# A hybrid mLSTM and gated DeltaNet block on one core: the sums of u tied to the weight splits, a quarter of an inverse copied out first and read a step later, one mLSTM head started three steps later

## The chip, the cores and the metric

One core of one Trainium2 chip runs the kernel. The metric is device microseconds from the first to the last work of a launch, the median of several runs. The engines named below are PE (TensorE, matrix products into PSUM banks), DVE (VectorE), ACT (ScalarE), POOL (GpSimd) and SP (SyncE, which here only issues DMAs; ACT issues some too). Each engine works through its own instructions in order and waits on semaphores for the others.

## The reference, cut to what matters

Sequence 512, model width 2048, one layer. A normalised input u is multiplied by one wide weight matrix; its columns feed two token mixers and their gates.

```python
u = _rmsnorm(h, norm_w)
proj = jnp.matmul(u, w_in)          # (512, 2048) x (2048, 20528)
...
h_a = _mlstm_chunkwise(q, k, v, i_pre, logf)          # 8 heads, q/k 128 wide, v 256 wide
h_a = _merge_heads(_rmsnorm(h_a)) * ml_norm_w * sigmoid(ml_o) * silu(ml_z)
...
h_b = _gated_delta_chunkwise(dq, dk_, dv_, beta, g)   # 16 heads, 128 wide
#   per chunk: lhs = I + strict_lower(beta * (k k^T) * decay); sol = lhs^-1 rhs
h_b = _merge_heads(_rmsnorm(h_b, dn_norm_w)) * silu(dn_z)
y = sigmoid(gate_a) * (h_a @ w_out[:2048]) + sigmoid(gate_b) * (h_b @ w_out[2048:])
out = _rmsnorm(x + y, final_norm_w)
```

All of it is float32. The inverse of a unit lower triangular matrix per head and chunk (`lhs`) is what the second part of the change touches.

## The kernel before, in words

**Products in three.** Each float32 operand is split into a high part rounded to the matrix unit's float32r and a low remainder, and a product is three matmuls: high by high, high by low, low by high. u is kept split (`uh`, `ul`). Weights come from memory in steps: `load_raw` (SP) brings `wr`, `split_hi` (ACT, line 135) casts it to `wh`, `split_lo` (DVE, line 138) subtracts to `wl`. Four buffers of each; splits are made three steps ahead (`SAHEAD`), with the priority offset 2 x `PRIO`.

**Order.** PE's instructions stay in the order in which the program writes them. The other engines' are ordered by a scheduler that simulates time: an instruction that is ready may be pulled ahead of ones written earlier, and `urgent(level)` lifts its priority by level x `PRIO`. `behind("V")` and `behind("A")` place an instruction after the newest weight split of DVE or ACT that had been written by then. They add an order on that engine, no semaphore.

**Ticks.** `proj_cm` and `proj_tm` are the projections. After every 6 matmuls of 512 columns (12 of 256 in `proj_tm`) they call `tick()`, which advances a clock by one and lets background generators run: each generator writes some work, yields a number, and comes back that many ticks later. `start(gen, wait)` sets its first tick. So a number in a `yield` or `start` places work between the projection's matmuls. A projection of 256 columns takes 16 ticks.

**First stage.** After the first projection (ML_Q) the generators `gates()`, `u_sums()` (start 9) and `lead()` start, beside ML_K and two narrow gate projections (48 ticks in all; their results leave PSUM by ACT in `spill`, line 369, and `narrow_gates`, line 733, at ticks 16, 32 and 48). `u_sums` runs eight iterations: DVE adds `uh` and `ul` of two row blocks into `X` (line 391), POOL makes four sums and differences (lines 394 to 397), four ticks later ACT casts them to `suh` and `s4h` (line 400) and DVE subtracts to `sul` and `s4l` (line 401), one tick later the next iteration begins. There is one `X`. The sums are read by the next stage.

**Seven products.** A stage of wide projections (`seven`, lines 586 to 588) uses a scheme of seven products in place of eight for 2 x 2 blocks, with `suh`, `sul`, `s4h`, `s4l`, and takes until about 990 us.

**Units.** Eight units then run, each with two DeltaNet heads and, in units 1 to 6, an mLSTM head (`dn_unit`): projections DN_K, for these units the mLSTM's q and k, DN_V and DN_Q, 16 ticks each. Evacuations of the projections' banks (`yp`, line 777) are ACT's. mLSTM heads 0 and 1 have their q and k computed earlier, and `ml_first(0)` and `ml_first(1)` start at ticks 1 and 42 of this stage. A head loads q and k (`mkq`, one buffer), turns k by a DVE transpose and a trip through memory (`turn`, `travel`: four small DMAs out, lines 803 to 818), loads its broadcast rows and v (line 1110, one buffer `v1`), works through four chunks and stores its result to `hm_d` by eight DMAs that ACT issues (line 813).

**The inverse.** `dn_front_k` inverts the 32 x 32 diagonal blocks; `dn_back` joins them for eight matrices at a time (two heads, four chunks):

- p1 (line 944), copied out negated to `s1` by ACT (line 949), two ticks;
- p2 (lines 955 and 956), three groups in one PSUM bank. ACT copies two of them to `tb` (line 960), then DVE copies the third to `ta` (line 962); two ticks;
- p3 (line 966) reads `ta`; ACT negates it to `s3` (line 969); two ticks;
- p4 (line 973) reads `s3` and `tb`; DVE copies it to `tb` (line 975); then two chains (`dn_chain`) start, which run the recurrence with `tb`.

Accesses of different engines to one PSUM bank are ordered one after the other, as written. `dn_back` starts 9 ticks after the unit's last projection, 25 in the units without an mLSTM head.

**End.** Two more gate projections, then the output projection, in which the stored results are read back.

Of the kernel before, what the change touches and what calls it, by code (L numbers as in the profile page):

```python
# [8 lines left out]
F32 = mybir.dt.float32  # L9
F32R = mybir.dt.float32r  # L10
AF = mybir.ActivationFunctionType
ALU = mybir.AluOpType
# [4 lines left out]
S = 512  # L17
# [13 lines left out]
HP = S // 2  # L31
# [24 lines left out]
def hybrid_body(  # L56
# [18 lines left out]
    V, A, G, T = nc.vector, nc.scalar, nc.gpsimd, nc.tensor  # L75
# [64 lines left out]
    def behind(eng):  # L140

        return tc.issue_after(newest[eng])
# [70 lines left out]
    def urgent(level=1):  # L213
        return tc.high_priority(offset=level * PRIO)
# [4 lines left out]
    def start(gen, wait=0):  # L219
        active.append([gen, clock["t"] + wait])  # L220
# [12 lines left out]
    uh = up.tile([P, KT, S], F32R, tag="uh", name="uh")  # L233
    ul = up.tile([P, KT * S + 120], F32R, tag="ul", name="ul")[:, 0:KT * S].rearrange("p (k s) -> p k s", s=S)
# [149 lines left out]
    X = sbp.tile([P, 2, 2, NO], F32, tag="X", name="X")  # L384
    U1, C22 = ([X[:, q, t, :] for t in range(2)] for q in range(2))
    t2_d = dr.tile([2, KH, P, NO], F32, tag="t2d", name="t2_d")

    def u_sums():
        for i in range(KH):
            uf, sf = X[:, 0, :, :], X[:, 1, :, :].rearrange("p a (b n) -> p (a b) n", n=HP)  # L390
            V.tensor_tensor(out=uf, in0=uh[:, 2 * i:2 * i + 2, :].bitcast(F32), in1=ul[:, 2 * i:2 * i + 2, :].bitcast(F32),
                            op=ALU.add)
            a11, a21, a12, a22 = uf[:, 0, 0:HP], uf[:, 0, HP:S], uf[:, 1, 0:HP], uf[:, 1, HP:S]
            G.tensor_tensor(out=sf[:, 0], in0=a21, in1=a22, op=ALU.add)
            G.tensor_tensor(out=sf[:, 1], in0=sf[:, 0], in1=a11, op=ALU.subtract)
            G.tensor_tensor(out=sf[:, 2], in0=a11, in1=a21, op=ALU.subtract)
            G.tensor_tensor(out=sf[:, 3], in0=a12, in1=sf[:, 1], op=ALU.subtract)
            yield 4
            for hi, lo, src in ((suh[:, i], sul[:, i], sf[:, 0:3]), (s4h[:, i], s4l[:, i], sf[:, 3])):
                A.copy(hi, src)  # L400
                V.tensor_tensor(out=lo, in0=src, in1=hi.bitcast(F32), op=ALU.subtract)
            yield 1

    acol = cp.tile([P, NC, MLH], F32, tag="acol", name="acol")
# [314 lines left out]
    def lead():  # L719
        for _ in range(3):  # L720
            load_quad()
            yield 2
        prep_sums(0)
        prep_pair(0)
        yield 1
# [8 lines left out]
            nc.sync.dma_start(tg_d[2 * i:2 * i + 2, :, b * NB:(b + 1) * NB].rearrange("c p n -> p c n"), tg)  # L734

    start(gates())
    start(u_sums(), 9)
    start(lead(), 38)
    spill(proj_cm(ML_K), 2, 1.0)
    for b in range(GFIRST):  # L740
# [20 lines left out]
    ta = wk.tile([64, 2 * NC, 64], F32, tag="ta", name="ta", bufs=1)  # L761
# [8 lines left out]
    def bc(col, n):  # L770
        return col.unsqueeze(2).to_broadcast([P, NC, n])
# [158 lines left out]
    def dn_back(hs, kq, u):  # L930

        tn, tt = u["tn"], u["tt"]
        G2 = [(j * NC + c, u["aq"][j][:, c, 0, :]) for j in range(2) for c in range(NC)]
        for b in range(4):
            bs = slice(b * BS, (b + 1) * BS)
            G.tensor_copy(tb[bs, :, bs], tt[bs])
        for b in range(2):
            bs = slice(b * BS, (b + 1) * BS)
            G.tensor_copy(ta[bs, :, bs], tn[bs])
        p1 = psw.tile([P, 2 * NC, BS], F32, tag="wk", name="p1")  # L940
        for g, a in G2:
            for q in range(2):
                a0, a1 = slice(64 * q, 64 * q + 32), slice(64 * q + 32, 64 * q + 64)
                T.matmul(p1[a1, g, :], a[a0, a1], tn[a0, g, :], start=True, stop=True)
        s1 = wk.tile([P, 2 * NC, BS], F32, tag="s3", name="s1", bufs=1)
        for q in range(2):
            a1 = slice(64 * q + 32, 64 * q + 64)
            with urgent():
                A.mul(s1[a1], p1[a1], -1.0)
        yield 2  # L950
        p2 = psw.tile([P, 2, 2 * NC, BS], F32, tag="wk", name="p2")
        for g, a in G2:
            for q in range(2):
                a0, a1 = slice(64 * q, 64 * q + 32), slice(64 * q + 32, 64 * q + 64)
                T.matmul(p2[a0, 0, g, :], s1[a1, g, :], tt[a1, g, :], start=True, stop=True)
            T.matmul(p2[32:64, 1, g, :], tt[32:64, g, :], s1[32:64, g, :], start=True, stop=True)
        for q in range(2):
            a0, a1 = slice(64 * q, 64 * q + 32), slice(64 * q + 32, 64 * q + 64)
            with urgent():
                A.copy(tb[a0, :, a1], p2[a0, 0])  # L960
        with urgent():
            V.tensor_copy(ta[32:64, :, 0:32], p2[32:64, 1])
        yield 2
        p3 = psw.tile([P, 2 * NC, 64], F32, tag="wk", name="p3")
        for g, a in G2:
            T.matmul(p3[64:128, g, :], a[0:64, 64:128], ta[:, g, :], start=True, stop=True)
        s3 = wk.tile([P, 2 * NC, 64], F32, tag="s3", name="s3", bufs=1)
        with urgent():
            A.mul(s3[64:128], p3[64:128], -1.0)
        yield 2  # L970
        p4 = psw.tile([P, 2 * NC, 64], F32, tag="wk", name="p4")
        for g, a in G2:
            T.matmul(p4[0:64, g, :], s3[64:128, g, :], tb[64:128, g, 64:128], start=True, stop=True)
        with urgent():
            V.tensor_copy(tb[0:64, :, 64:128], p4[0:64])
        for j in range(2):
            vn = u["vs"][j]
            with behind("V"):
                V.tensor_tensor(out=vn, in0=vn, in1=bc(u["nk"][:, j, :], P), op=ALU.mult)
        start(dn_chain(0, hs, kq, u), 2)  # L980
        start(dn_chain(1, hs, kq, u), 3)
# [60 lines left out]
    def dn_unit(p, mh):  # L1042
# [27 lines left out]
        for j in range(2):  # L1070
# [3 lines left out]
            start(silu_end(kq[j][:, 1, :], (kq[j][:, 1, :], qn)), 4 + 3 * j)  # L1074
        start(dn_front_q(hs, kq, u), QWAIT)
        start(dn_back(hs, kq, u), 25 if mh is None else 9)

    def ml_head(h, kq, late):
# [83 lines left out]
    def ml_first(h):  # L1162

        kq = wk.tile([P, 2, S], F32, tag="mkq", name="mkq", bufs=1)
        for i in range(2):
            nc.sync.dma_start(kq[:, 1 - i, :], qk_d[2 * i + h])
        yield 4
        yield from ml_head(h, kq, 0)

    start(ml_first(0), 1)  # L1170
    start(ml_first(1), 42)
    for unit in UNITS:
        dn_unit(*unit)

# [137 lines left out]
def hybrid_block(tc, *args):  # L1312
    with tc.block(schedule_with_timeline_sim=True):
        hybrid_body(tc, *args)
# [25 lines left out]
```

## Time and profile before

| | us |
|---|---|
| median of 3 runs | 2259.2 (2257.6 to 2261.88) |
| the profiled execution, its own time | 2272.74 |
| its span, first to last instruction | 2271.0 |
| PE busy | 2200.4 |
| DVE busy | 1581.6 |
| ACT busy | 917.9 |
| POOL busy | 264.1 |

The page gives one execution under the hardware profiler. "Busy" is the union of an engine's instructions; waiting and the issue of DMAs are not busy. A row of the timeline reads: start in us from the span's start, duration in us, engine and line, operation, what it writes and reads, shape and count, and in brackets the idle time of that engine just before it with what ended it. In the view of waits a row reads: who waited for whom, total us, how often, the longest. A row of the windows gives the stretch, its length, the busy time of PE, of PE's weight loads, of DVE, ACT and POOL with their instruction counts, the clock granted to TensorE, the share of the DMA engines and GB/s. A `q` behind an engine's name is its sequencer, here the issue of a DMA.

### The profile page before, as it was taken

To read this page: it belongs to the slowest core of one execution; us is meant where nothing else is said; L and a number is where in the kernel's file an instruction comes from. 1 tells how busy PE (TensorE), PEld (TensorE's weight loads), DVE (VectorE), ACT (ScalarE), POOL (GpSimd) and SP (SyncE) were. 2 spreads that over 40 slices of the span, in tenths; PEclk is the share of its full clock that TensorE was granted. 3 is DMA by queue.
4 is the path that set the end of the run, shared out by engine and by line. 5 is a ranking of instruction groups with operands and counts; after the bars stand their busy time and mean duration, and the time that the engine had idled before them with its cause. 6 is when DMAs were issued, how large, how long until landed. Compare 5 with 4: busy or idle time off the path is not lost.

```text
span 2271.0 us, 33013 instructions
## 1 busy us (share of the span) xinstructions
PE 2200.4 (97%) x11504; PEld 1842.8 (81%) x11504; DVE 1581.6 (70%) x2793; ACT 917.9 (40%) x1788; POOL 264.1 (12%) x340
## 2 busy tenths in 40 slices
PE   6899999999999999999999999999999999999998
PEld 5887888788778778887888878787878899978886
DVE  5967798788778777757877777776777775444435
ACT  4434444445444444443434334343434434332223
POOL 0500000000000000012312121212121210000111
PEclk9999999999999999999999999999999999999999
DMA  5355666567667766867666665656565566864333
GB/s 158 87 190 184 205 208 209 191 199 229 202 206 220 232 205 201 250 189 186 154 155 160 143 156 140 156 140 150 142 153 141 143 165 181 251 200 148 116 116 130
DMA packets 521385, 397.09 MB, mean 175 GB/s; under 512 B 239873, under 2 KB 408034, under 8 KB 521218
## 3 DMA queue, kind: packets, MB, share of 16 engines
q1 hardware_dynamic: 427778, 341.42, 53.9%
q10 hardware_dynamic: 93440, 53.56, 7.8%
q8 instruction: 90, 1.47, 0.3%
q14 instruction: 77, 0.63, 0.1%
HBM read 318.25 MB, written 76.61 MB: 174 GB/s over the span
## 4 chain that ended last, share of the span: by engine, by line
PE 64%; DMA 17%; DVE 10%; issue 3%; SPq 3%; ACT 2%; POOL 0%; ACTq 0%; DVEq 0%; POOLq 0%
PE pj L258 9%; PE pj L259 9%; PE pj L260 9%; PE ps L587 6%; PE ps L586 6%; PE ps L588 6%; DMA wr<-t_d 5%; DVE wl L138 5%; PE py L1274 3%; PE py L1275 3%; PE py L1273 3%; DMA wr<-in_w_in_dram 3%; DMA hm_d<-to 2%; SPq L512 1%; ACT wh L135 1%
## 5 line engine op out<-in xcount | busy, mean ns | idle before, releaser
L138 DVE TENSOR_TENSOR wl<-wr,wh 128x512 fp32r<-128x512 f32 (+1 forms) x592 | 480.0, 814 | 271.1 <-ACT wh L135 265.6
L135 ACT CAST wh<-wr 128x512 fp32r<-128x512 f32 (+1 forms) x592 | 404.0, 685 | 613.0 <-PE pj L259 240.9
L258 PE MATMUL pj<-uh,wh 128*128 128x512 f32 x1024 | 433.3, 423 | 4.9 <-ACT yp L777 4.9
L260 PE MATMUL pj<-uh,wl 128*128 128x512 f32 x1024 | 404.0, 395 | 0.0
L259 PE MATMUL pj<-ul,wh 128*128 128x512 f32 x1024 | 403.1, 394 | 0.0
L260 PEld LDWEIGHTS pj<-uh,wl 128*128 128x128 f32 x1024 | 194.4, 190 | 44.1
L258 PEld LDWEIGHTS pj<-uh,wh 128*128 128x128 f32 x1024 | 195.4, 191 | 40.9 <-ACT yp L777 5.7
L259 PEld LDWEIGHTS pj<-ul,wh 128*128 128x128 f32 x1024 | 195.7, 191 | 33.5
L587 PE MATMUL ps<-wl,uh 128*128 128x512 f32 x528 | 208.1, 394 | 6.7 <-DVE wl L138 6.5
L586 PE MATMUL ps<-wh,uh 128*128 128x512 f32 x528 | 207.1, 392 | 4.8 <-DVE X L567 4.6
L586 PE MATMUL ps<-wh,suh 128*128 128x512 f32 x528 | 205.8, 390 | 1.4 <-ACT to L626 1.4
L588 PE MATMUL ps<-wh,ul 128*128 128x512 f32 x528 | 205.7, 390 | 0.0
L587 PE MATMUL ps<-wl,suh 128*128 128x512 f32 x528 | 205.5, 389 | 0.0
L588 PE MATMUL ps<-wh,sul 128*128 128x512 f32 x528 | 205.4, 389 | 0.0
L135 ACT CAST wh<-ts 128x512 fp32r<-128x512 f32 x176 | 109.0, 619 | 201.3 <-DVE ts L542 154.4
L135 ACT CAST wh<-t 128x1024 fp32r<-128x1024 f32 x88 | 92.9, 1055 | 196.0 <-PE ps L588 108.6
L273 PE MATMUL pjt<-wh,uh 128*128 128x256 f32 x512 | 148.5, 290 | 4.2 <-ACT tgs L733 2.7
L275 PE MATMUL pjt<-wl,uh 128*128 128x256 f32 x512 | 145.9, 285 | 1.8 <-DVE wl L138 1.8
L276 PE MATMUL pjt<-wh,ul 128*128 128x256 f32 x512 | 145.6, 284 | 0.0
L138 DVE TENSOR_TENSOR wl<-ts,wh 128x512 fp32r<-128x512 f32 x176 | 120.4, 688 | 33.7 <-ACT wh L135 33.7
L138 DVE TENSOR_TENSOR wl<-t,wh 128x1024 fp32r<-128x1024 f32 x88 | 107.8, 1225 | 43.8 <-ACT wh L135 43.2
L587 PEld LDWEIGHTS ps<-wl,uh 128*128 128x128 f32 x528 | 99.1, 188 | 35.1 <-DVE wl L138 16.0
(288 smaller groups left out, 3897.9 us busy)
## 6 DMA issues: line engine op xcount, KB each, us to landing
wr<-in_w_in_dram SPq DMA_DIRECT2D x680, 256.0 KB, 3.7
wr<-in_w_out_dram SPq DMA_DIRECT2D x128, 256.0 KB, 3.1
t_d<-ts ACTq DMA_DIRECT2D x88, 256.0 KB, 3.9
wr<-t_d SPq DMA_DIRECT2D x88, 256.0 KB, 4.1
wr<-in_w_in_dram SPq DMA_DIRECT2D x96, 128.0 KB, 2.8
tgl<-tg_d SPq DMA_DIRECT2D x24, 256.0 KB, 3.9
xt<-in_x_dram SPq DMA_DIRECT2D x8, 512.0 KB, 7.7
v<-v_d SPq DMA_DIRECT2D x8, 512.0 KB, 6.8
```

The costliest lines, as they stand in the source:

```text
L135: newest["A"] = A.copy(hi, src).ins
L138: newest["V"] = V.tensor_tensor(out=lo, in0=src, in1=hi.bitcast(F32), op=ALU.subtract).ins
L258: T.matmul(ps[j], hi[:, k, wsl], uh[:, kt, :], start=(kt == 0), stop=False)
L259: T.matmul(ps[j], hi[:, k, wsl], ul[:, kt, :], start=False, stop=False)
L260: T.matmul(ps[j], lo[:, k, wsl], uh[:, kt, :], start=False, stop=(kt == KT - 1))
L273: T.matmul(o, uh[:, kt, tsl], hi[:, k, :], start=(kt == 0 and c % 2 == 0), stop=False, skip_group_check=True)
L275: T.matmul(o, uh[:, kt, tsl], lo[:, k, :], start=False, stop=False, skip_group_check=True)
L276: T.matmul(o, ul[:, kt, tsl], hi[:, k, :], start=False, stop=(kt == KT - 1), skip_group_check=True)
L586: T.matmul(ps[t], ah, hi, start=(g == "A" and i == 0), stop=False, skip_group_check=True)
L587: T.matmul(ps[t], ah, lo, start=False, stop=False, skip_group_check=True)
L588: T.matmul(ps[t], al, hi, start=False, stop=(i == KH - 1), skip_group_check=True)
L1273: T.matmul(ps[c], hh[base][:, kt, tsl], hi[:, 0, :], start=(kt == 0), stop=False)
```

## The change

Three edits. In `u_sums` the DVE and ACT instructions are put behind the newest weight split of their engine, the views of `X` are made once, and the generator starts at tick 11 in place of 9. In `dn_back` the copy of `ta` is written ahead of ACT's two copies from the same bank, with the priority offset 2 x `PRIO` in place of one, and p3 comes three ticks after p2 in place of two. The second mLSTM head starts at tick 45 in place of 42.

```diff
     def u_sums():
+        uf, sf = X[:, 0, :, :], X[:, 1, :, :].rearrange("p a (b n) -> p (a b) n", n=HP)
+        a11, a21, a12, a22 = uf[:, 0, 0:HP], uf[:, 0, HP:S], uf[:, 1, 0:HP], uf[:, 1, HP:S]
         for i in range(KH):
-            uf, sf = X[:, 0, :, :], X[:, 1, :, :].rearrange("p a (b n) -> p (a b) n", n=HP)
-            V.tensor_tensor(out=uf, in0=uh[:, 2 * i:2 * i + 2, :].bitcast(F32), in1=ul[:, 2 * i:2 * i + 2, :].bitcast(F32),
-                            op=ALU.add)
-            a11, a21, a12, a22 = uf[:, 0, 0:HP], uf[:, 0, HP:S], uf[:, 1, 0:HP], uf[:, 1, HP:S]
+            with behind("V"):
+                V.tensor_tensor(out=uf, in0=uh[:, 2 * i:2 * i + 2, :].bitcast(F32),
+                                in1=ul[:, 2 * i:2 * i + 2, :].bitcast(F32), op=ALU.add)
             G.tensor_tensor(out=sf[:, 0], in0=a21, in1=a22, op=ALU.add)
...
             yield 4
             for hi, lo, src in ((suh[:, i], sul[:, i], sf[:, 0:3]), (s4h[:, i], s4l[:, i], sf[:, 3])):
-                A.copy(hi, src)
-                V.tensor_tensor(out=lo, in0=src, in1=hi.bitcast(F32), op=ALU.subtract)
+                with behind("A"):
+                    A.copy(hi, src)
+                with behind("V"):
+                    V.tensor_tensor(out=lo, in0=src, in1=hi.bitcast(F32), op=ALU.subtract)
             yield 1
...
-    start(u_sums(), 9)
+    start(u_sums(), 11)
...
             T.matmul(p2[32:64, 1, g, :], tt[32:64, g, :], s1[32:64, g, :], start=True, stop=True)
+        with urgent(2):
+            V.tensor_copy(ta[32:64, :, 0:32], p2[32:64, 1])
         for q in range(2):
             a0, a1 = slice(64 * q, 64 * q + 32), slice(64 * q + 32, 64 * q + 64)
             with urgent():
                 A.copy(tb[a0, :, a1], p2[a0, 0])
-        with urgent():
-            V.tensor_copy(ta[32:64, :, 0:32], p2[32:64, 1])
-        yield 2
+        yield 3
         p3 = psw.tile([P, 2 * NC, 64], F32, tag="wk", name="p3")
...
     start(ml_first(0), 1)
-    start(ml_first(1), 42)
+    start(ml_first(1), 45)
```

## The prediction

> **What bounds the kernel now.** I read the page first.
>
> ```profile
> span 2271.0 us, 33013 instructions
> PE 2200.4 (97%) x11504; PEld 1842.8 (81%) x11504; DVE 1581.6 (70%) x2793; ACT 917.9 (40%) x1788; POOL 264.1 (12%) x340
> ```
>
> PE is the bound: of 2271.0 us it idles 70.6. The change removes no matmul, so it can only move PE's waits and what follows from them. Second, PE's waits, longest in total first.
>
> ```profile
> engine line waited for: us in total, times, longest us
> PE p L966 <- DVE ta L962: 13.3, 5, 3.6
> PE pj L258 <- ACT yp L777: 4.9, 1, 4.9
> PE pjt L273 <- ACT tgs L733: 2.7, 1, 2.7
> PE pjt L275 <- DVE wl L138: 1.8, 2, 1.4
> PE pjt L273 <- ACT qk L369: 1.5, 1, 1.5
> ```
>
> L966 is the product p3 of the inverse, which waits for the quarter `ta`. L273 and L275 are the narrow projections that run beside the sums of u. L258 behind L777 is one wait near 1077 us, beside the second mLSTM head. So each part of the change stands beside one of the largest waits. Third, TensorE's granted clock (third figure from the end, 1.00 being full) in windows laid around these waits, and matmul steps from the chain in the second window.
>
> ```profile
> 110.00:118.00 8.00, 5.66 (x29) 5.66 (x30) 3.66 (x9) 3.89 (x8) 0.83 (x2) 0.57 0.58 153
> 1076.00:1084.00 8.00, 6.26 (x16) 4.97 (x17) 6.28 (x15) 4.02 (x9) 0.26 (x1) 0.57 1.11 233
> 1329.00:1333.00 4.00, 4.00 (x12) 2.87 (x10) 1.90 (x3) 0.78 (x2) 0.00 (x0) 0.57 0.77 202
> 1441.00:1446.00 5.00, 5.00 (x22) 3.71 (x19) 1.88 (x4) 1.21 (x2) 0.00 (x0) 0.66 0.91 215
> 1554.00:1562.00 8.00, 7.96 (x43) 6.25 (x44) 2.79 (x5) 1.90 (x4) 0.99 (x1) 0.57 1.01 253
> 1670.00:1674.00 4.00, 4.00 (x21) 3.25 (x19) 0.40 (x2) 1.21 (x2) 0.00 (x0) 0.57 0.93 226
> 1082.80 0.43 PE pj L260
> 1084.25 0.23 PE pj L259
> ```
>
> After each long wait the clock is lowered for a while and a matmul step takes 0.43 us in place of 0.23. A window of 8 us at 0.57 misses 8 x 0.43 = 3.4 us of clock; at half clock a missed microsecond costs (1 - 0.23/0.43)/0.5 = 0.93 us, so 3.2 us. The four windows from 1329 miss 1.7 + 1.7 + 3.4 + 1.7 = 8.5 us: 8.0 us of time. The waits above therefore cost more than their own row tells.
>
> **The quarter that leaves first.** The third product's starts, and the stretch around the second of them:
>
> ```profile
> 1327.36 0.82 PE L966 MATMUL p<-ta,aq 64*64 64x64 f32 x11 [2.77 <-DVE ta L962]
> 1440.42 0.76 PE L966 MATMUL p<-ta,aq 64*64 64x64 f32 x10 [2.89 <-DVE ta L962]
> 1554.04 1.25 PE L966 MATMUL p<-ta,aq 64*64 64x64 f32 x12 [3.44 <-DVE ta L962]
> 1669.60 0.59 PE L966 MATMUL p<-ta,aq 64*64 64x64 f32 x7 [3.60 <-DVE ta L962]
> 1434.39 0.19 PE L956 MATMUL p<-s,tt 32*32 32x32 f32 x1
> 1436.38 1.53 DVE L138 TENSOR_TENSOR wl<-wr,wh 128x512 fp32r<-128x512 f32 x1 [3.07 <-ACT wh L135]
> 1436.81 2.24 ACTq L813 DMA_DIRECT2D hm_d<-to  x3
> 1439.09 0.74 ACT L960 COPY tb<-p 32x256 f32<-32x256 f32 x2 [2.74 <-DMA hm_d<-to]
> 1439.86 0.42 DVE L962 COPY ta<-p 32x256 f32<-32x256 f32 x1 [1.95 <-ACT tb L960]
> ```
>
> p2 is complete at 1434.6. ACT is held in its issues of hm_d, copies tb only at 1439.09, and DVE's copy of ta, from the same bank and later in the program, waits for ACT's two. With ta first, ACT waits for DVE instead. But DVE has a weight split (1436.38 to 1437.91) ahead of it, itself held by ACT; both rank alike for the scheduler and the split is the older, so I leave it first: ta is then done at 1437.91 + 0.42 = 1438.3. PE's place for p3, without the wait, is 1440.42 - 2.89 = 1437.5. The third step of the yield adds one tick, six matmul steps of 0.23, 1.4 us: 1438.9. So p3 finds ta there with 0.6 us to spare; the reorder alone would leave some 0.8 us of wait. The other three units read alike, by their waits. At once behind the tb copies on ACT stand one hm_d issue, a weight cast and s3's evacuation, and p4 waits for the last: p3 ends at 1438.9 + 1.1 = 1440.0 (estimate from 16 products), p4's place is two ticks on, 1442.8, and ACT is done with tb at 1439.83, so after that issue and the cast s3 still has some 1.5 us (estimate). p4, the copy back and the chains all move one tick; PE fills that tick with projection products, so it costs nothing while these last, and 1.4 us at the most behind the last unit, where gate products still run. Removed: 13.3 us of waits plus 8.0 us of lowered clock, 21.3; bounds 8 (half of the waits stay, the clock with them partly) and 21.3. I take 21.
>
> Row against rule: gaps of 2.77 and 2.89 us were each followed by the lowered clock (windows from 1329 and 1441). The Trainium skill (TensorE: Matmul & The Clock Gate, Part 1: The HAM clock gate) has the clock halved after at least one idle window of about 3.4 us, by which these two gaps would have kept the full clock. By that rule alone the sum would be 3.2 us smaller; the trace decides, and I use its windows.
>
> **The sums of u.** First what ACT waited for ahead of line 400, then rows of the timeline:
>
> ```profile
>   POOL X L395: 21.6, 7
> 80.59 0.83 ACT L400 CAST suh<-X 128x768 fp32r<-128x768 f32 x1 [3.81 <-POOL X L395]
> 59.00 0.74 POOL L396 TENSOR_TENSOR X<-X 128x256 f32<-128x256 f32 x1
> 103.93 1.21 DVE L391 TENSOR_TENSOR X<-uh,ul 128x1024 f32<-128x1024 f32 x1
> 106.08 2.66 POOL L394 TENSOR_TENSOR X<-X 128x256 f32<-128x256 f32 x1 [2.62 <-DVE sul L401]
> 110.14 0.83 ACT L400 CAST suh<-X 128x768 fp32r<-128x768 f32 x1 [1.64 <-POOL X L395]
> 111.70 0.59 ACT L733 ACTIVATE tgs<-pjt 128x512 f32<-128x512 f32 x1
> ```
>
> The first row is ACT's idle time ahead of its casts of these sums: seven waits, 21.6 us. They run far ahead of the step that wrote them: the free scheduler pulled them forward, and ACT and DVE, in order, then stand in front of PE's evacuations. At 80.59 that held qk (1.5 us of PE), at 110.14 it held tgs (2.7 us, then the lowered clock of 110 to 118, 3.2 us). Tied to the splits, an iteration starts with its tick (11, 16, ... 46) and casts four ticks later (15, ... 50); the evacuations are at ticks 16, 32 and 48. Four ticks of about 1.4 us are 5.6 us; the slowest iteration shown, DVE add at 103.93 to ACT cast at 110.14, took 6.2, the first POOL sums 0.74 each. So most casts find their data. The DVE, ACT and POOL instructions are the same in number; they end 15 to 20 us later (tick 50 in place of 111), beside the first strips of the seven-product stage, which reads one iteration's sums every four ticks, about 5.5 us, and so the last one's long after tick 50. What is queued behind a tied cast is the next weight cast, and PE waits for that. All that could go: 2.7 + 1.5 + 1.8 + 3.2 = 9.2; it could also give 3 us back at the new overlap (one wait like tgs). I take 6.5: qk, tgs and its clock gone (7.4), the wl waits kept, 0.9 for the overlap.
>
> **The second head.** The timeline around the yp wait, and in the second row the chain:
>
> ```profile
> 1071.24 0.43 SPq L1110 DMA_DIRECT2D v<-v_d  x1
> 1071.24 5.49 DMA v<-v_d
> 1073.21 3.85 ACTq L813 DMA_DIRECT2D hm_d<-to  x2
> 1077.10 0.59 ACT L777 COPY yp<-pj 128x512 f32<-128x512 f32 x1 [5.86 <-DMA v<-v_d]
> 1075.30 4.22 SPq L813 DMA_DIRECT2D td<-kw  x4
> ```
>
> The first head's hm_d issues on ACT wait for the landing of the second head's v, and the evacuation yp stands behind them. Of the second head's transfers on SP, the two mkq loads were issued ahead of this stretch, v goes when the first head frees its buffer, which three ticks (4.1 us) of trace order do not alter, and td of kw, tied to a split, moves to about 1079.4. That takes four transfers out of the stretch, but they were issued after v. All of it could go (4.9 + 3.2 = 8.1), or a wait could arise at the third head, whose one mkq buffer is freed one tick before it is wanted (1.4 us lost). I take 2.
>
> **Sum.** 21 + 6.5 + 2 = 29.5; I take off 2 for waits that newly come up, since everything that ran during the stalls now has less time: 27.5. The profiled execution took 2272.74 us (span 2271.0 and 1.7 around it): 2245 after. The median of the runs shown is 2259.2, 13.5 lower. If these 13.5 lie in PE's 70.6 idle us, the waits are a fifth smaller there and the gain is 22; if not, 27.5. I take 25: 2234.
>
> **Rivals.**
> 1. The wait moves rather than goes: DVE's ta copy stays behind a split whose cast stands behind ACT's hm_d issues. The 0.6 us to spare speaks for it; the tick given as well speaks against it. With 2 us left in each of four units and their clock lowered as now, 21 becomes 5 and the sum 5 + 6.5 + 2 - 2 = 11.5, scaled 10: 2249. Chance 0.18.
> 2. POOL stays as slow where the sums are put: L394 took 2.66 us beside DVE's work and 0.74 is what L396 took, so casts go on waiting. The sums then gain nothing: 27.5 - 6.5 = 21, by the same scaling 19, 2240. Chance 0.14. Beside this: the Trainium skill (SBUF — State Buffer, Who interferes with whom) has a DVE instruction with two SBUF inputs and a GpSimd one that reads SBUF exclude each other for a whole instruction. No row here shows whether it is that lock.
> 3. The second head's three steps do clear the v collision: 8.1 in place of 2, and the wl waits go as well: about 35 by the profile, 32 scaled, 2227. For it: the stretch has fewer transfers; against it: v's issue time. Chance 0.08.
> 4. Slower: the tied casts hold the weight casts on ACT, so PE waits in each of the eight iterations. Like tgs with its clock, 2.7 + 3.2 = 5.9 each, 47; less 9.2 that go and 23 of the other parts: 15 slower, 2274. It decides from (23 + 9.2)/8 = 4.0 us an iteration. A weight cast runs about three steps of 2.7 us (twelve of 0.23) ahead of its use, so POOL would have to end some 8 us later than in the slowest iteration shown, and in every one. Chance 0.05.
>
> **How the numbers follow.** Forecast 0.53 (2222 to 2243), rivals 0.18, 0.14, 0.08, 0.05, and 0.02 that nothing measurable happens. 0.2% (4.5 us) is about what a measurement tells from no change. A part of rival 1 and of rival 2 ends within it: faster 0.87, same 0.07, slower 0.06. The range reaches from all that could go (21.3 + 9.2 + 8.1 = 38.6, less 2 for new waits and unscaled, 37) to a gain of 8, the low bound of the quarter alone: 2222 to 2251.
>
> **What would show it.** L966 behind L962 gone from PE's waits, or under 3 us; the granted clock full near 1330, 1440, 1550 and 1670; ta's copy ahead of tb's; tgs and qk gone from PE's waits and the clock full at 110 to 118; ACT's idle time ahead of L400 well under 21.6. The yp wait near 1075 may stay. Wrong would be: p3 still waiting 2 us or more, p4 (L973) taking its place, or weight splits (L138) as PE's largest wait before 180 us.

## The result, and the profile after

| | before | after |
|---|---|---|
| median, us | 2260.58 (6 runs, 2257.6 to 2268.12) | 2241.63 (6 runs, 2234.45 to 2244.56) |
| ratio, 95% interval | | 0.9904 [0.988, 0.9928] |
| the profiled execution, us | 2272.74 | 2236.92 |
| PE idle in it (span less PE busy), us | 70.6 | 46.9 |

The change makes the kernel 19 us faster by the medians; 25 were forecast, 2234 against 2241.63. The two profiled executions lie 35.9 us apart by their spans, since that of before stands 12 us above its median and that of after 5 below. Of the 35.9, 23.7 are idle time of PE that went (70.6 - 46.9) and 12.2 are busy time (2200.4 - 2188.2) with the same 11504 matmuls. The clock accounts for most of these: the six windows of the prediction miss 15.3 us of clock in all, after has only the yp window below at 0.57 (3.4 us), and 11.9 us at the prediction's 0.93 are 11.1 us of time (estimate). Of the idle time, 19.3 us are the rows at which the change aims (below); another 5.5 are waits in the seven products, to which the paragraph on the sum comes back. The first rows of the page of after:

```profile
span 2235.1 us, 33004 instructions
PE 2188.2 (98%) x11504; PEld 1835.7 (82%) x11504; DVE 1566.5 (70%) x2793; ACT 913.6 (41%) x1788; POOL 271.6 (12%) x340
```

The waits of PE in after (who waited for whom, total us, how often, the longest):

```profile
...
PE pj L258 <- ACT yp L780: 4.5, 1, 4.5
PE ps L589 <- DVE X L570: 2.9, 4, 1.2
PE ps L590 <- DVE wl L138: 2.7, 6, 0.5
```

Lines after the first edit are three higher now: p3 is L969, p4 L976, the evacuation yp L780, the seven products L589 and L590. The wait of p3 for `ta` (13.3 us) is no row any more, nor are `tgs`, `qk` and the weight split of the narrow gates (6.0 together). The yp wait stays. Above it stands only that of the kernel's first product (`pprm`), 15.0 us and 15.1 in before, which the change doesn't touch; below it come waits of a size that before had too. The same places by windows in after (stretch, length, busy PE, PEld, DVE, ACT, POOL, granted clock, DMA share, GB/s): beside the sums, at the yp wait, and round p3 of the four units whose p3 waited longest in before (it now starts at 1307.76, 1417.13, 1526.53 and 1635.06).

```profile
110.00:118.00 8.00, 8.00 (x69) 8.00 (x69) 7.22 (x9) 3.86 (x6) 4.30 (x4) 1.00 0.79 288
1059.00:1067.00 8.00, 5.54 (x14) 4.45 (x15) 5.56 (x12) 2.31 (x4) 0.00 (x0) 0.57 1.05 241
1303.00:1311.00 8.00, 8.00 (x91) 6.52 (x84) 2.23 (x3) 2.28 (x5) 2.04 (x3) 1.00 0.88 157
1416.00:1424.00 8.00, 8.00 (x58) 6.29 (x57) 3.96 (x7) 4.05 (x8) 0.00 (x0) 1.00 0.86 175
1526.00:1534.00 8.00, 8.00 (x57) 6.35 (x56) 5.98 (x10) 4.15 (x8) 0.63 (x1) 1.00 0.91 230
1634.00:1642.00 8.00, 8.00 (x58) 6.32 (x57) 5.65 (x10) 4.15 (x8) 0.23 (x1) 1.00 0.82 204
```

Five of the six are at full clock, with PE never idle in them. Only the yp window is still at 0.57, and elsewhere in after the clock is lowered only behind the last matmul, from 2227 on. How the quarter passes now is read from the timeline of after in the same unit as the prediction's (start, duration, engine and line, operation, idle time before it):

```profile
1413.64 1.53 DVE L138 TENSOR_TENSOR wl<-wr,wh 128x512 fp32r<-128x512 f32 x1 [2.02 <-ACT wh L135]
1415.20 0.42 DVE L961 COPY ta<-p 32x256 f32<-32x256 f32 x1
1415.50 3.05 ACTq L816 DMA_DIRECT2D hm_d<-to  x4
1418.59 0.74 ACT L965 COPY tb<-p 32x256 f32<-32x256 f32 x2 [4.98 <-DMA hm_d<-to]
1419.35 1.14 ACT L135 CAST wh<-wr 128x512 fp32r<-128x512 f32 x2
1420.52 0.59 ACT L972 ACTIVATE s<-p 64x512 f32<-64x512 f32 x1
1417.13 1.14 PE L969 MATMUL p<-ta,aq 64*64 64x64 f32 x16
1421.17 1.14 PE L976 MATMUL p<-tb,s 64*64 64x64 f32 x16
```

DVE copies `ta` directly behind the weight split, at 1415.62 it is done, and p3 starts 1.5 us later. ACT is held by its hm_d issues as before (4.98 us idle), but now only `tb` and `s3` come late from it, and p4 needs them four microseconds after p3. `s3` ends at 1421.11 and p4 starts at 1421.17: it just fits.

### The profile page after: what moved, and what is told of

It reads as the page before. It is cut to its first block, busy times and chain, and to the rows that moved or that the text cites. A ratio compares the mean times of both kernels' runs of the same rounds, so it can differ in the third digit from the quotient of the medians.

```text
span 2235.1 us, 33004 instructions
## 1 busy us (share of the span) xinstructions
PE 2188.2 (98%) x11504; PEld 1835.7 (82%) x11504; DVE 1566.5 (70%) x2793; ACT 913.6 (41%) x1788; POOL 271.6 (12%) x340
## 4 chain that ended last, share of the span: by engine, by line
PE 74%; DMA 11%; DVE 8%; issue 3%; ACT 2%; SPq 2%; POOL 0%; DVEq 0%; ACTq 0%; POOLq 0%
PE pj L258 10%; PE pj L260 9%; PE pj L259 9%; PE ps L590 9%; PE ps L589 9%; PE ps L591 9%; PE py L1277 3%; PE py L1276 3%; PE py L1278 3%; DVE wl L138 3%; DMA wr<-t_d 3%; DMA wr<-in_w_in_dram 2%; DMA hr<-h_d 1%; ACT wh L135 1%; SPq L515 1%
## 5 line engine op out<-in xcount | busy, mean ns | idle before, releaser
L138 DVE TENSOR_TENSOR wl<-wr,wh 128x512 fp32r<-128x512 f32 (+1 forms) x592 | 479.8, 814 | 280.4 <-ACT wh L135 273.0
L589 PE MATMUL ps<-wh,uh 128*128 128x512 f32 x528 | 206.9, 392 | 3.5 <-DVE X L570 2.9
L590 PE MATMUL ps<-wl,uh 128*128 128x512 f32 x528 | 207.8, 394 | 2.5 <-DVE wl L138 2.2
L589 PE MATMUL ps<-wh,suh 128*128 128x512 f32 x528 | 205.7, 390 | 0.7 <-ACT to L629 0.6
L590 PE MATMUL ps<-wl,suh 128*128 128x512 f32 x528 | 205.6, 389 | 0.5 <-DVE wl L138 0.5
L275 PE MATMUL pjt<-wl,uh 128*128 128x256 f32 x512 | 144.7, 283 | 0.0
L138 DVE TENSOR_TENSOR wl<-ts,wh 128x512 fp32r<-128x512 f32 x176 | 120.9, 690 | 29.8 <-ACT wh L135 29.8
L138 DVE TENSOR_TENSOR wl<-t,wh 128x1024 fp32r<-128x1024 f32 x88 | 107.7, 1224 | 38.9 <-ACT wh L135 38.4
L590 PEld LDWEIGHTS ps<-wl,uh 128*128 128x128 f32 x528 | 99.1, 188 | 29.5 <-DVE wl L138 10.3
```

The costliest lines, as they stand in the source:

```text
L138: newest["V"] = V.tensor_tensor(out=lo, in0=src, in1=hi.bitcast(F32), op=ALU.subtract).ins
L275: T.matmul(o, uh[:, kt, tsl], lo[:, k, :], start=False, stop=False, skip_group_check=True)
L589: T.matmul(ps[t], ah, hi, start=(g == "A" and i == 0), stop=False, skip_group_check=True)
L590: T.matmul(ps[t], ah, lo, start=False, stop=False, skip_group_check=True)
```

## The experiments

Each kernel ran beside the kernel before on the same chip, in five rounds. The three groups of four ran on three chips, so kernels of different groups are compared by their ratios. The kernel before was at 2270.99 us (17 runs) beside the first four, 2268.97 (11 runs) beside the next four and 2268.23 (23 runs) beside the last four.

**The parts alone.** The first kernel has only the edit in the inverse:

```diff
+        with urgent(2):
+            V.tensor_copy(ta[32:64, :, 0:32], p2[32:64, 1])
         for q in range(2):
...
-        with urgent():
-            V.tensor_copy(ta[32:64, :, 0:32], p2[32:64, 1])
-        yield 2
+        yield 3
```

> The inverse's edit alone (ta copied first, p3 a step later), on the kernel before. Theory: it takes away PE's waits at p3 and the lowered clock behind them and is about two thirds of the gain of 19 us: 12 to 14 us faster, no p3 wait in PE's list, full clock near 1330, 1440, 1550 and 1670; the waits beside the sums of u (some 6 us) and the yp wait (4.9) stay. Rival (the wait moves on to p4 or the copies): 0 to 6 us faster, and p4 (L973) or its chain's first product stands in PE's waits with 2 us or more a unit.

Measured: 2249.8 us, ratio 0.9907 [0.989, 0.9924], 21 us. Its waits of PE:

```profile
PE pj L258 <- ACT yp L777: 5.2, 1, 5.2
...
PE pjt L273 <- ACT tgs L733: 2.9, 2, 2.7
PE pr L997 <- DVE st L1016: 2.6, 1, 2.6
...
PE pjt L273 <- ACT qk L369: 1.7, 1, 1.7
```

No row of p3 is left. The yp wait, `tgs` and `qk` stand, the weight splits of L275 are down to 0.4 us, and one of the chains (L997) comes up. The clock is at 1.00 in 8 us from each of the four p3 that waited before (windows from 1325, 1433, 1543 and 1651). So this edit alone removes the waits and the lowered clock that were put down to it; it gained more than the 12 to 14 us expected here and as much as the prediction took. The page can't be set against that gain, since the profiled execution (2260.18) is the slowest of the seven.

The second has only the sums of u: the tie to the splits, the views moved out of the loop, and the start.

```diff
+            with behind("V"):
+                V.tensor_tensor(out=uf, in0=uh[:, 2 * i:2 * i + 2, :].bitcast(F32),
+                                in1=ul[:, 2 * i:2 * i + 2, :].bitcast(F32), op=ALU.add)
...
+                with behind("A"):
+                    A.copy(hi, src)
+                with behind("V"):
+                    V.tensor_tensor(out=lo, in0=src, in1=hi.bitcast(F32), op=ALU.subtract)
...
-    start(u_sums(), 9)
+    start(u_sums(), 11)
```

> The edit of the sums of u alone (tied to the splits, start 11), on the kernel before. Theory: the waits for qk and tgs go and the clock stays full at 110 to 118, 5 to 7 us faster; the p3 waits stay at 13 us. Rival (POOL as slow elsewhere, casts still wait, a wait at the head of the seven-product stage): within 2 us of the kernel before.

Measured: 2258.92 us, ratio 0.9949 [0.993, 0.9967], 12 us. Its waits, and its window beside the sums:

```profile
PE p L969 <- DVE ta L965: 10.1, 5, 3.6
...
PE pj L258 <- ACT yp L780: 4.6, 1, 4.6
```

```profile
110.00:118.00 8.00, 8.00 (x69) 8.00 (x68) 7.45 (x8) 3.95 (x6) 4.84 (x4) 1.00 0.87 309
```

`tgs` and `qk` are gone and the clock beside them is full; p3 waits for 10.1 us in all, five times as before.

The third has only `start(ml_first(1), 45)` in place of 42.

> The second mLSTM head's three ticks alone, on the kernel before. Theory: v is loaded when its buffer comes free, so the yp wait of 4.9 us and its lowered clock stay: within 2 us of the kernel before. Rival (the three ticks thin out the transfers): the yp wait goes below 2 us, 5 to 8 us faster.

Measured: 2271.32 us (12 runs), ratio 0.9991 [0.9977, 1.0006]: no difference. The yp wait stays, one long wait as before:

```profile
PE p L966 <- DVE ta L962: 9.2, 5, 3.0
...
PE pj L258 <- ACT yp L777: 3.6, 1, 3.6
```

The fourth is the whole change with that one line put back to 42.

> The whole change without the head's three ticks (start 42). Theory: as the whole change, within 2 us of 19 us faster, yp wait between 4 and 5 us. Rival (the head's ticks matter once the other waits are gone): 5 us or more slower than the whole change, 14 us faster at the most, with a longer yp wait or a new wait around the third head's bank evacuations.

Measured: 2241.89 us, ratio 0.9881 [0.986, 0.9902]; 27 us by the ratio where 19 were expected; the yp wait 5.1 us, once. The head's three ticks can be left out with nothing lost that these runs can tell.

**The whole change again,** unaltered, beside the next kernels:

> The whole change again, beside the three that follow, on one chip. The change without the head's ticks was 27 us faster than the kernel before on another chip. Theory: the whole change is 0.9905 of the kernel before, and the difference to the one without the head's ticks lies within what two chips differ. Rival: the parts work against each other only with the head's ticks, and it stays at 0.992 or above.

Measured: 2245.88 us, ratio 0.9908 [0.9889, 0.9928]: the first result repeated.

**The two halves of the inverse's edit.** One kernel has the kernel before with `ta` copied first and `yield 2` kept:

```diff
+        with urgent(2):
+            V.tensor_copy(ta[32:64, :, 0:32], p2[32:64, 1])
         for q in range(2):
...
-        with urgent():
-            V.tensor_copy(ta[32:64, :, 0:32], p2[32:64, 1])
         yield 2
```

> On the kernel before, ta copied ahead of tb, but p3 two steps after p2 as before. Theory: DVE has ta some 0.8 us after PE reaches p3, so small waits, too short to lower the clock: 14 to 20 us faster, but p4 (L973) comes 1.4 us earlier to a negation that stands behind ACT's copies of tb and waits some 1 us a unit. Rival (the order does nothing, the extra step is what counts): p3 still waits 2 us or more in four units, at most 4 us faster.

Measured: 2252.59 us, ratio 0.9937 [0.9917, 0.9957]. Its waits:

```profile
PE p L966 <- DVE ta L958: 3.2, 4, 1.2
...
PE p L973 <- ACT s L969: 1.0, 2, 0.8
```

Four waits remain. The unit that the prediction had worked out keeps 0.96 us (p3 at 1426.34) against its 0.8. Of the three that it read alike, two keep 0.76 and 0.28 us and one keeps none. The longest, 1.22 us, is in the last unit (1862.05), which waited 0.56 in before and was not among its four. So their average of 0.8 us is chance. Nor does p4 wait 1 us in each unit, as expected, but 1.0 in all. The other kernel has the old order with `yield 3`:

```diff
-        yield 2
+        yield 3
```

> On the kernel before, p3 a step later, with ta still copied after tb. Theory: each wait of 2.8 to 3.6 us becomes 1.4 us shorter, 1.4 to 2.2 us are left in each of the four units, and the clock is lowered less often: 8 to 13 us faster, more than the 5.5 us that the waits alone give back. Rival (the step only moves the wait): within 4 us of the kernel before.

Measured: 2254.62 us, ratio 0.9942 [0.9921, 0.9963]. Its waits:

```profile
PE p L973 <- ACT s L969: 2.4, 1, 2.4
...
PE p L966 <- DVE ta L962: 1.9, 2, 1.3
```

Three of the five p3 waits vanish by the added step alone and two remain (0.62 and 1.30 us), where 1.4 to 2.2 us in each of four units were expected: how long ACT's issues hold `tb` differs from unit to unit. In the last unit a wait of p4 (2.4 us) takes the place of one of p3 (0.56 in before). Of the 13.3 us of p3 waits the order takes 10.1 and the step 11.4, more together than there are. So the halves overlap: either shortens the same wait, and what they save is the wait of p3 once, with the clock behind it. By their ratios they give 14 and 13 us and both together 21, which fits, though intervals of 4 to 5 us either way wouldn't show it by themselves.

**The sums: the tie or the start?** One kernel is that of the sums' edit alone with the old start:

```diff
-    start(u_sums(), 11)
+    start(u_sums(), 9)
```

> On the kernel before, the sums of u tied to the weight splits, but started at tick 9 as before. Theory: the tie is what keeps the sums from running ahead of PE's evacuations: most of the 5 to 12 us of the whole edit, with the waits for qk and tgs gone or short (an iteration's cast now falls on the ticks 13, 18, ... 33, 48, one of them on an evacuation's own tick, so one wait of 1 to 2 us may stay). Rival (the later start is what counts): within 3 us of the kernel before.

The other is the kernel before with the new start and no tie:

```diff
-    start(u_sums(), 9)
+    start(u_sums(), 11)
```

> On the kernel before, the sums of u started at tick 11, without the tie. Theory: the scheduler pulls them forward all the same, the waits for qk (1.5 us) and tgs (2.7) and the lowered clock stay: within 3 us of the kernel before. Rival: the start alone clears one of the two, 4 us or more faster.

Measured: the tie alone 2262.13 us (12 runs), ratio 0.9968 [0.9955, 0.998]; the start alone 2270.04 us (12 runs), ratio 1.0012 [0.9996, 1.0028]. The window beside the sums, with the tie alone:

```profile
110.00:118.00 8.00, 8.00 (x69) 8.00 (x68) 6.68 (x10) 3.85 (x6) 2.35 (x3) 1.00 0.82 296
```

The same window with the start alone, then the last of the eight DVE adds in its timeline:

```profile
110.00:118.00 8.00, 5.52 (x26) 5.52 (x27) 3.65 (x9) 3.89 (x8) 0.97 (x2) 0.57 0.59 170
```

```profile
104.06 1.21 DVE L391 TENSOR_TENSOR X<-uh,ul 128x1024 f32<-128x1024 f32 x1
```

Untied, a start two ticks later moves nothing: the last add runs at 104.06, in before at 103.93, and the clock is 0.57 in both. The scheduler pulls the work forward in any case. The tie is what takes effect, and it alone clears the window. Whether the later start adds something once the tie is there isn't settled: 7 us (5 to 10) with the tie alone and 12 (7 to 16) with both, on two chips.

**What the yp wait hangs on.** In after the timeline of SP and ACT shows the old picture, 16 us earlier; behind it stand two rows of the chain, the load from its issue to its landing and the third of the three hm_d issues:

```profile
1054.85 0.43 SPq L1113 DMA_DIRECT2D v<-v_d  x1
...
1056.82 3.96 ACTq L816 DMA_DIRECT2D hm_d<-to  x3
1060.82 0.58 ACT L780 COPY yp<-pj 128x512 f32<-128x512 f32 x1 [5.24 <-DMA v<-v_d]
```

```profile
1054.85 5.54 DMA v<-v_d
...
1060.47 0.31 ACTq L816
```

A store that ACT issues waits until a load that SP issued has landed (1054.85 + 5.54 = 1060.39), though it neither reads nor writes what that load touches. The 3.96 us of the row above cover three issues; the second ends at 1058.07, so this load holds the third for 2.4 us. The trace's semaphore events name the reason: the DMAs of both queues take turns on eight completion semaphores, and this hm_d issue comes next on the one that the load of v still holds (number 107, whose last update from the load is at 1060.39). The evacuation stands behind it on ACT. If so, it helps to issue v elsewhere, not to start the head later. The whole change with v's load put behind SP's newest weight load:

```diff
...
-                nc.sync.dma_start(raw, src.rearrange("(k p) n -> p k n", p=P))
+                newest["S"] = nc.sync.dma_start(raw, src.rearrange("(k p) n -> p k n", p=P)).ins
...
-        nc.sync.dma_start(v1[:, :, 0:NB], v_d[:, :, h * NB:(h + 1) * NB].rearrange("c p n -> p c n"))
+        with behind("S"):
+            nc.sync.dma_start(v1[:, :, 0:NB], v_d[:, :, h * NB:(h + 1) * NB].rearrange("c p n -> p c n"))
```

> The whole change, with the mLSTM heads' loads of v issued by SP behind the newest weight load instead of as soon as their buffer is free. Theory: the yp wait near 1061 us comes from hm_d issues that wait on ACT for the landing of the second head's v; with v later the wait falls below 2 us and its lowered clock goes, 4 to 8 us faster than the whole change. Rival (the small packets of hm_d and the other loads fill the transfer engines anyway): the wait stays at 4 us and so does the time.

Measured: 2240.3 us, ratio 0.9889 [0.9865, 0.9913]. Its waits, a window round the place, and two rows of its timeline:

```profile
PE pnum L1126 <- DVE c L1134: 2.3, 1, 2.3
...
PE pj L258 <- ACT yp L780: 1.8, 1, 1.8
```

```profile
1060.00:1068.00 8.00, 6.24 (x28) 4.84 (x27) 7.13 (x22) 2.63 (x5) 0.00 (x0) 1.00 1.09 271
```

```profile
1063.40 0.59 ACT L780 COPY yp<-pj 128x512 f32<-128x512 f32 x1 [3.08 <-DMA hm_d<-to]
...
1072.66 0.47 SPq L1114 DMA_DIRECT2D v<-v_d  x1
```

v goes 18 us later, the wait falls from 4.5 (5.4 in the repeated whole change) to 1.8 us, and the clock there stays full. ACT is still held in issuing its stores: by the semaphore events, the one just ahead of this evacuation waits for a weight load of SP (landed at 1062.97). And a new wait of 2.3 us comes up where the head's second chunk needs the state that DVE copies from the first (L1126). It is no wait for v: the head's first product runs at 1092.76, in after at 1092.56. The median is 5.6 us under that of the whole change on the same chip, with intervals that overlap. Two more kernels: the same with the head back at tick 42, and the same as the former (tick 45) with the two loads of `mg` behind the weight load as well.

```diff
-    start(ml_first(1), 45)
+    start(ml_first(1), 42)
```

> The change without the head's ticks (start 42) and with v's load tied behind the newest weight load. Theory: the head's ticks bring nothing, the tie takes the yp wait: 0.987 to 0.990 of the kernel before, as the whole change with the tie (0.9889), yp wait under 2 us. Rival (the ticks are what makes room for the tie): the yp wait stays above 4 us and the ratio above 0.991.

```diff
-                    nc.sync.dma_start(g[i], g_d[:, :, col:col + P].rearrange("c p n -> p c n"))
+                    with behind("S"):
+                        nc.sync.dma_start(g[i], g_d[:, :, col:col + P].rearrange("c p n -> p c n"))
```

> The whole change with v's load and the two loads of the gate rows mg tied behind the newest weight load. Theory: with v gone from the stretch the rest of the yp wait (1.8 us) comes from the mg loads, 512 KB issued beside hm_d: the wait goes below 1 us, and the time is 0.986 to 0.989 of the kernel before. Rival (the later mg loads are then late for the head's last product): a new wait of DVE or POOL for mg, and no gain over v alone (0.9889) or a loss.

Measured: with the head at 42, 2241.75 us (4 runs), ratio 0.9884 [0.9865, 0.9904], yp wait 2.4 us; with `mg` moved too, 2245.39 us, ratio 0.9898 [0.988, 0.9917], yp wait 1.4 us and these waits in the head's chunks:

```profile
PE pnum L1126 <- DVE c L1134: 2.8, 1, 2.8
...
PE pnum L1126 <- DVE c L1136: 1.8, 4, 0.7
```

So v's load as the cause of most of the yp wait is shown by the cut to 1.4 to 2.4 us in three kernels. The rest doesn't come from `mg` alone: with `mg` moved too, under 1 us and a gain were expected; 1.4 us and no gain over v alone were measured, and the store just ahead of the evacuation still waits for another load of SP (landed at 1063.75). That removing the wait pays isn't shown. In the two versions with the head at 45 a new wait of the head comes up, whose tie to the move of v is not shown either; with the head at 42 it doesn't, but there the ratio is the same with v moved (0.9884) and without (0.9881). No version's interval lies clear of the whole change's.

## Why the prediction was right, and where it was off

**The quarter (21 taken).** Right in size and way: 21 us alone. The order of DVE came out, p3 has time to spare (0.6 forecast, 1.5 in after), and the order alone leaves 0.96 us in the unit for which 0.8 were worked out. One detail was off: 1.5 us were left for `s3`, and after has 0.06 (1421.11 to 1421.17), since ACT's issues held `tb` until 1418.59. That it cost nothing hung on some tenths; the kernel with the old order and the new step shows the wait that lies there (p4, 2.4 us).

**The clock behind short gaps.** The forecast set the trace's windows above the rule of the Trainium skill (TensorE: Matmul & The Clock Gate, Part 1: The HAM clock gate), at least one idle window of about 3.4 us, and the runs bear that out: even a gap of 1.22 us was followed by a lowered clock, where the expectation of that run had called such waits too short. In the kernel with the order alone, a row of the timeline and the window round it:

```profile
1862.05 0.41 PE L966 MATMUL p<-ta,aq 64*64 64x64 f32 x4 [1.22 <-DVE ta L958]
```

```profile
1860.00:1868.00 8.00, 6.78 (x53) 6.41 (x53) 5.69 (x10) 4.89 (x9) 0.00 (x0) 0.79 0.62 184
```

0.79 over 8 us is 8 x 0.21 x 2 = 3.4 us at half clock; before showed 6.9 (0.57 over 8 us) or 3.4. The rule's own length, about 3.4 us, does appear, as the length of the lowered stretch. But a gap of its own size isn't needed, and a short one isn't always enough. In after, the longest wait but for the yp one and that of the first product, in the timeline and the window round it:

```profile
1985.27 0.50 PE L1276 MATMUL py<-wh,uh 128*128 128x512 f32 x1 [1.60 <-ACT wh L135]
```

```profile
1983.00:1991.00 8.00, 6.17 (x26) 4.51 (x25) 3.88 (x6) 3.19 (x6) 0.00 (x0) 1.00 0.53 171
```

1.60 us idle, and the clock stays at 1.00. What decides between such gaps is not settled by these runs.

**The sums (6.5 taken).** Right in way, mis-sized: 12 us alone (interval 7 to 16, from 1 - 0.9967 and 1 - 0.993 of 2270.99), above the 9.2 that the rows gave as the most. The rows explain 9.2 of it, and the rest lies within the interval. A part of it can be clock behind `qk`: the profile of before shows none there, but in the inverse's kernel alone, where `qk` holds PE for 1.7 us, the window behind it is lowered, which by the same sum is another 1.6 us (estimate):

```profile
80.00:88.00 8.00, 6.28 (x40) 6.07 (x40) 7.83 (x15) 3.36 (x6) 4.47 (x6) 0.79 0.48 137
```

The overlap with the seven products, for which 0.9 was held back, cost little: their waits up to 190 us are 2.2 us in after and 0.8 in before. The casts of the sums in after, by lines (busy us, mean ns, then ACT's idle time ahead of them and what ended it):

```profile
L402 ACT CAST suh<-X 128x768 fp32r<-128x768 f32 x8 | 6.7, 832 | 8.1 <-POOL X L396 8.1
```

8.1 us in place of 21.6.

**The head (2 taken).** Nothing: 0.9991 [0.9977, 1.0006]. The reason given for taking little was right, v's issue hangs on the buffer and not on the tick; then the term should have been 0.

**The sum (27.5) and its scaling to 25.** This is the step that missed most. Alone, the parts give 21 + 12 + 2 = 35 us by their ratios; all together give 22 and, repeated, 21 (19 and 23 by the medians), and the change without the head's ticks 27 (22 to 32). So the 2 us taken off for waits that newly come up were too few, or the parts overlap; with intervals of 3 to 5 us either way on each, it isn't settled which. What is seen is that waits of the seven products swing between executions of one and the same code: 5.6 us for L589 and L590 in after's profile (2.9 + 2.7), 9.7 in that of the repeat (3.4 + 6.3). In before they were 11.1, two rows that the prediction's list of the longest waits passes over without a mark, as it does that of `pprm`:

```profile
PE ps L587 <- DVE wl L138: 6.5, 12, 1.4
...
PE ps L586 <- DVE X L567: 4.6, 7, 1.7
```

So the 5.5 us between the two profiles can't safely be put down to the change. The scaling took the profiled 2272.74 for a run out of the common. Among the later runs of the kernel before (2256.74 to 2280.09) it is an ordinary one, and the three first shown were low (whether by their chip is not on record). The scaling brought the number nearer, by a reason that the later runs don't bear out. So the nearness of 25 is in part luck: the parts alone give some 5 us more than was forecast for them (35 against 29.5) and lose 13 together, where 4.5 were taken off.

**The rivals.** A wait that only moves (2249) fell: p3 waits for nothing in after. POOL as slow as before (2240) is the nearest in number, nearer than the forecast, and wrong in its way. POOL is slow in places, as the timeline of after shows by the slowest sum and DVE's instructions meanwhile,

```profile
122.20 2.79 POOL L395 TENSOR_TENSOR X<-X 128x256 f32<-128x256 f32 x1 [6.51 <-DVE X L393]
121.98 1.21 DVE L138 TENSOR_TENSOR wl<-t,wh 128x1024 fp32r<-128x1024 f32 x1
123.11 0.68 DVE L138 TENSOR_TENSOR wl<-ts,wh 128x512 fp32r<-128x512 f32 x1
123.72 0.68 DVE L138 TENSOR_TENSOR wl<-wr,wh 128x512 fp32r<-128x512 f32 x1
```

and yet the sums gained 12 us alone: ACT now meets them later, and waits 8.1 us for them. The sum starts under a weight split and ends at 124.99, 0.6 us after the third (124.40). All 32 sums in after divide so: 0.73 to 0.74 us where DVE ran no instruction with two inputs from SBUF at their start (17 of them), 0.85 to 2.79 us where it did. That is how the lock would look of which the Trainium skill tells (SBUF — State Buffer, Who interferes with whom); no run took DVE's part away, so it isn't proved. The head that clears the collision of v fell (4.5 us remain). Slower, by tied casts that hold the weight casts, fell too: PE has no idle moment from 110 to 118, and in the seven products L138 costs 2.7 us in all, 0.5 at the most, of it 1.0 us before 190.

## What to carry to other kernels

A copy that one product waits for should be the first out of its bank and on the engine that isn't held by DMA issues; a tick of distance or the order each gives some two thirds of that alone (13 and 14 of 21 us), and after both the next user of the held engine (here `s3`) has the slack to be watched. Background work that a scheduler may pull forward is placed by an order on its engine, not by its start: a later start alone moved nothing here, the tie alone cleared the waits. If PE waits for an evacuation on an engine that also issues DMAs, look which landing its issue waits for; but moving one load left the issue to wait for the next one's landing, and no gain in time was shown here for a wait cut from 4.5 to 1.8 us.

## What the runs showed of the hardware

- TensorE's clock halved after idle gaps of 1.22, 2.77 and 2.89 us, for stretches of about 3.4 or 6.9 us (0.79 or 0.57 over 8 us), while a gap of 1.60 us passed without. By the prediction's price the clock behind the wait of 1.22 us cost another 1.6 us (estimate: 1.7 us of clock missed, at 0.93 us each).
- A DMA issue on ACT was held for 2.4 us, from 1058.07 to 1060.47, for the landing of a load from SP with which it shares only a completion semaphore.
- POOL's sum of 128x256 took 0.73 to 0.74 us where DVE ran no instruction with two inputs from SBUF at its start, and 0.85 to 2.79 us where it did (32 sums of after).
- Medians of one unchanged kernel in four sets of runs lay 10 us apart (0.46%), half of the gain that was to be measured.
